# A DiT step on one core: the tiles that matmuls stream are placed at multiples of 64 bytes in SBUF

## The chip, the core and the metric

The kernel runs on one core of one Trainium2 chip, and nothing else runs on the other cores. The metric is device time in microseconds (us) of one launch. The time before is 2669.81 us, the median of 3 runs (2667.17 to 2671.09). TensorE (PE in the profile) multiplies. VectorE (DVE), ScalarE (ACT) and GpSimd (POOL) do the elementwise work. Every DMA is issued from SyncE's queue (SP). SBUF is the on-chip memory with 128 partitions. "The address" of a tile below is the byte in each partition at which it starts.

## What is computed

One layer of a diffusion backbone works on 128 context tokens and 2048 latent tokens of width 1024, everything in float32. The parts that matter here are the input projection and the MLP.

```python
def block(x, s0, mod, ...):
    sh1, sc1, ga1, sh2, sc2, ga2 = mod
    h = rmsnorm(x, norm_mix_l) * (1.0 + sc1) + sh1
    o, s_new = mixer(h, s0, n_chunks, w_in_l, ...)   # h @ w_in, conv, DeltaNet scan, gMLP, @ w_out
    x = x + ga1 * o
    h = rmsnorm(x, norm_ffn_l) * (1.0 + sc2) + sh2
    x = x + ga2 * (jnp.square(jax.nn.relu(h @ w_ff1_l)) @ w_ff2_l)   # 1024 -> 4096 -> 1024
    return x, s_new
```

A final RMSNorm follows. The outputs are both token streams and the last DeltaNet states.

## The kernel before

**Products.** TensorE multiplies float32 data in the type fp32r, in one pass. To keep float32 precision, both operands are split into a high and a low part, and `mm3` (lines 221 to 227) issues three matmuls for each product: high by high (L225), high by low (L226), low by high (L227). In `T.matmul(ps, a, b)` the tile `a` is loaded into the array as the stationary operand, and the tile `b` is streamed. The profile writes a matmul as `out<-streamed,stationary`, so `f<-hop,zH` streams a tile called `hop` past the stationary tile `zH`, and `pj<-kH,wH` streams `kH` past `wH`.

**Stages.** By the first matmuls of each kind in the profile's timeline there are four stages.

- Up to about 520 us, the input projection for q, k and v in feature layout. Tokens go in six blocks: block 0 has 388 columns, blocks 1 to 4 have 386, block 5 has 258. `prep_block` makes for each of the 8 slices of the width a tile `kH` and a tile `kL` (lines 483 and 484): the modulated rows, high and low part. `feature_tile` streams their first 388, 386 or 258 columns against the weights `wH`, `wL`, and `ab_block` (L625, L626) streams them against `abW`.
- From there to 1279 us, the DeltaNet scan, its triangular inverses in float16 (`unit`, L1041 to L1120), the gMLP and the output projection. The tiles of the inverses (`AH`, `X`, `Y`, `P`, `R`) lie in the pool `prep`.
- From 1279.42 to 1991 us, the first MLP product. Rows and columns are combined in the way of Strassen, so that 7 block products take the place of 8. The order is `ORDER = (1, 5, 6, 7, 3, 2, 4)`. `Unit.product` (L1526) issues for each of 32 units and each product 4 x 3 matmuls that stream one `hop` tile: four runs of 128 columns, 4 KB apart.
- From 1991.11 us to the end, the second MLP product, again with 7 products. Each output unit `u` goes through four quarters `q` of the inner dimension, each quarter with one `hop` tile and 4 x 3 matmuls of 512 columns in a row (the loop at L1874).

**Where the tiles lie.** Two pools hold the `hop` tiles, which are 16 KB per partition. `hopA` has 2 of them at the right end of SBUF, where the pool `prep` lay before it (`swap_right`, L1355); `hopB` has 5 of them, just behind the pool `wp`. `hop_tile` (L932) chooses the pool:

```python
def hop_tile(dt, n):
    side, bufs = ("A", 2) if n else ("B", 5)
```

In the first MLP product, products 1 and 5 use hopA (L939: `o in ORDER[:2]`). In the second, of the 28 `hop` tiles that are built one after another, the first two of every five use hopA (L1649). Those are quarters 0 and 1 of the first product, 1 and 2 of the second, 2 and 3 of the third, 3 of the fourth, 0 of the fifth, 0 and 1 of the sixth, 1 and 2 of the last.

A tile's room is rounded up to 32 bytes. A `kH` or `kL` tile of 388 columns has 1552 bytes and takes 1568, which is 24.5 times 64, so every second one starts 32 bytes past a multiple of 64. The right end of SBUF itself lies 32 bytes past a multiple of 64, and so does every tile of hopA and of `prep`. In the built program the addresses, taken modulo 64, are:

| tiles | before | after |
|---|---|---|
| `hop` of hopA (2 places; 16 of the 42 streamed `hop` tiles) | 32 | 0 |
| `hop` of hopB (5 places; 26 of the 42) | 0 | 0 |
| `kH`, `kL` of block 0 | 0, 32 | 0, 0 |
| `kH`, `kL` of blocks 1 to 4 | half of the tiles 0, half 32 | 0, 0 |
| `kH`, `kL` of block 5 | 32, 0 | 0, 0 |
| `AH`, `AL`, `X`, `Y`, `P`, `R`, `E`, `Es`, `KK` of `prep` | 32 | 0 |
| `wsT`, a stationary operand (L1248) | 32 | 0 |
| everything in `wp`, the other streamed tiles | 0 | 0 |

The two places of hopA are bytes 196576 and 212960 before, 196544 and 212928 after. Those of hopB are 113024, 129408, 145792, 162176 and 178560 in both.

The order of the instructions on each engine is worked out when the kernel is built.

Of the kernel before, what the change touches and what calls it, by code (L numbers as in the profile page):

```python
# [8 lines left out]
F32 = mybir.dt.float32  # L9
F32R = mybir.dt.float32r  # L10
# [7 lines left out]
P = 128  # L18
# [44 lines left out]
def hybrid_step(  # L63
# [11 lines left out]
    def xrow(t):  # L75
        return x_prompt[0] if t == 0 else x_sample[0, (t - 1) * P : t * P, :]
# [7 lines left out]
    def f32(ap):  # L84
        return ap.bitcast(F32)

    cp = ctx.enter_context(tc.tile_pool(name="const", bufs=1))
# [19 lines left out]
    def by_tiles(dst, tiles):  # L107

        return dst[tiles].rearrange("a p d -> p a d")
# [8 lines left out]
    make_identity(nc, ident)  # L118
    ident16 = cp.tile([P, P], F16, name="ident16")
    V.tensor_copy(ident16, ident)  # L120
    nhalf = cp.tile([P, 72], F32, name="nhalf")
    V.memset(nhalf, -0.5)
    zcol = cp.tile([P, KT], F32, name="zcol")
    V.memset(zcol, 0.0)
# [42 lines left out]
    wsT = cp.tile([P, 4, P], F32, name="wsT")  # L167
    scond = cp.tile([P, KT, 2], F32, name="scond")

    smp = ctx.enter_context(tc.tile_pool(name="small", bufs=4, reuse_waits="tile"))  # L170
    wp = ctx.enter_context(tc.tile_pool(name="wp", bufs=49, reuse_waits="tile"))
    wst = ctx.enter_context(ExitStack())
# [5 lines left out]
    def rsqrt_cols(out, ss, n, scale, eps):  # L178
        t = smp.tile([P, 72], F32, tag="rsq", name="rsq", bufs=2)
        np_ = ss.shape[0]  # L180
        V.tensor_scalar(out=t[:np_, :n], in0=ss, scalar1=scale, scalar2=eps, op0=ALU.mult, op1=ALU.add)  # L181
        G.tensor_tensor(out=out, in0=t[:np_, :n], in1=nhalf[:np_, :n], op=ALU.pow)  # L182
# [43 lines left out]
            T.matmul(ps, lh, rl, start=False, stop=False, skip_group_check=more)  # L226
            T.matmul(ps, ll, rh, start=False, stop=last and i == n - 1, skip_group_check=more)  # L227

    pick = smp.tile([P, 2, 2], F32, tag="pick", name="pick", bufs=1)
    V.memset(pick, 0.0)  # L230
    V.memset(pick[:, 0, 0:1], 1.0)
    V.memset(pick[:, 1, 1:2], 1.0)
# [42 lines left out]
    with ExitStack() as ph:  # L275
        p1 = ph.enter_context(tc.tile_pool(name="p1", bufs=2, reuse_waits="tile"))
# [7 lines left out]
        def pt():  # L284
            return ppt.tile([P, 512], F32, tag="pt", name="pt", bufs=3)
# [139 lines left out]
        def prep_block(bi):  # L425

            tiles = BLOCKS[bi]
            n = len(tiles) * P
            if bi == 0:
                ncol, segs = 388, [(1, 0, P, 0), (131, P, 2 * P, 1)]  # L430
            else:
                ncol, segs = n + 2, [(1, 0, n, 1)]
            hH, hL = [], []
            c0 = tiles[0] * P
            xs = []

            def load_x(t):
                if bi == 0:
                    xs.append(xs0[t])
                    return  # L440
                x = p1.tile([P, D], F32, tag="x", name="x", bufs=3)
                load(out=x, in_=xrow(t))
                if t == tiles[0]:
                    xs.append(smp.tile([P, 3], F32, tag="ss3", name="xss"))
                i = t - tiles[0]
                junk = p1.tile([P, D], BF16, tag="junk", name="junk", bufs=1)
                A.activation(junk, x, AF.Square, accum_out=xs[0][:, i : i + 1])

            def columns_r():
                nt = len(tiles)  # L450
                r = smp.tile([P, 3], F32, tag="rk", name="xr")
                rsqrt_cols(r[:, :nt], xs[0][:, :nt], nt, 1.0 / D, EPS)
                diag = p1.tile([P, 3, P], F32, tag="diag", name="diag", bufs=1)
                V.tensor_tensor(out=diag[:, :nt, :], in0=ident.unsqueeze(1).to_broadcast([P, nt, P]),
                                in1=r[:, :nt].unsqueeze(2).to_broadcast([P, nt, P]), op=ALU.mult)
                xs.append(diag)

            def rows_r():

                pr = pt()  # L460
                T.matmul(pr[:, :n], ones, xs[1][:, : len(tiles), :].rearrange("p a b -> p (a b)"), start=True,
                         stop=True)
                xs[1] = p1.tile([P, 384], F32, tag="rrow", name="rrow", bufs=1)
                A.copy(xs[1][:, :n], pr[:, :n])

            pairs = []

            def load_pair(j):
                x = p1.tile([P, D], F32, tag="x", name="xT", bufs=3)
                x = x[:, : 2 * n].rearrange("p (k t) -> p k t", k=2)  # L470
                load(out=x, in_=x_columns.rearrange("(k p) t -> p k t", p=P)[:, 2 * j : 2 * j + 2, c0 - P : c0 - P + n])
                pairs.append(x)

            zc, hc = [], []
            if bi == 0:
                zc, hc = [0, 129, 130], [(387, 1)]
            elif bi == 5:
                zc, hc = [n + 1], [(0, 8)]
            else:
                hc = [(0, 2 * bi - 2), (n + 1, 2 * bi + 1)]  # L480
            def column(k):
                full = p1.tile([P, 384], F32, tag="full", name="full", bufs=2)
                kH = p1.tile([P, 388], F32R, tag="h", name="kH", bufs=24)
                kL = p1.tile([P, 388], F32R, tag="h", name="kL", bufs=24)
                for col in zc:
                    G.tensor_copy(kH[:, col : col + 1], zcol[:, 0:1])
                    G.tensor_copy(kL[:, col : col + 1], zcol[:, 0:1])
                for col, j in hc:
                    G.tensor_copy(kH[:, col : col + 1], f32(halH)[:, k, j : j + 1])
                    G.tensor_copy(kL[:, col : col + 1], f32(halL)[:, k, j : j + 1])  # L490
                if bi == 0:
                    ps = pt()
                    for i, x in enumerate(xs):
                        T.transpose(ps[:, i * P : (i + 1) * P], x[:, k * P : (k + 1) * P], ident)
                    for s, o, m, cd in segs:
                        A.activation(full[:, o : o + m], ps[:, o : o + m], AF.Identity,
                                     scale=a1[:, cd, k : k + 1], bias=b1[:, cd, k : k + 1])
                    for s, o, m, _ in segs:
                        V.tensor_copy(kH[:, s : s + m], full[:, o : o + m])
                        V.tensor_tensor(out=kL[:, s : s + m], in0=full[:, o : o + m], in1=f32(kH)[:, s : s + m],  # L500
                                        op=ALU.subtract)
                else:
                    if k == 2:
                        load_pair(3)
                    b = b1[:, 1, k : k + 1]
                    V.scalar_tensor_tensor(out=full[:, :n], in0=pairs[k // 2][:, k % 2, :], scalar=a1[:, 1, k : k + 1],
                                           in1=xs[1][:, :n], op0=ALU.mult, op1=ALU.mult)
                    A.activation(kH[:, 1 : n + 1], full[:, :n], AF.Identity, bias=b)
                    V.scalar_tensor_tensor(out=kL[:, 1 : n + 1], in0=full[:, :n], scalar=b,
                                           in1=f32(kH)[:, 1 : n + 1], op0=ALU.add, op1=ALU.subtract)  # L510
                for s, o, m, _ in segs:
                    at = slice(tiles[0] + o // P, tiles[0] + (o + m) // P)
                    for dst, src in ((hH_d, kH), (hL_d, kL)):
                        store(out=by_tiles(dst[:, :, k, :], at),
                              in_=f32(src)[:, s : s + m].rearrange("p (a d) -> p a d", d=P))
                hH.append(kH)
                hL.append(kL)
            blk = (hH, hL, ncol, segs)
            first = [lambda t=t: load_x(t) for t in tiles]
            if bi:  # L520
                first += [lambda: (columns_r(), load_pair(0)), lambda: (rows_r(), load_pair(1)), lambda: load_pair(2)]
            return blk, first, [lambda k=k: column(k) for k in range(KT)]

        def feature_tile(blk, bi, gi, h):
# [250 lines left out]
        side = []  # L775
        for bi in range(len(BLOCKS)):
# [8 lines left out]
            for n, (gi, h) in enumerate(order):  # L785
# [40 lines left out]
                side = []  # L826
# [117 lines left out]
    with ExitStack() as ph:  # L944
        right = ctx.enter_context(ExitStack())
# [928 lines left out]
    for m, (n, i, u, q) in enumerate(todo):  # L1874
# [12 lines left out]
        h, lo = sops.pop(m)  # L1887
# [70 lines left out]
```

## Time and profile before

| | |
|---|---|
| time, median of 3 runs | 2669.81 us (2667.17 to 2671.09) |
| span of the profiled execution | 2670.2 us |
| mean granted TensorE clock | 0.994 |
| PE busy | 98% |
| PEld (weight loads, beside the matmuls) busy | 82% |
| DVE, ACT, POOL busy | 67%, 47%, 9% |
| DMA queue, share of 16 engines | 67.1% |

In the rows of the profile, `| 376.5, 393 | 1.2 <-ACT zH L1474 1.2` means 376.5 us busy in all, 393 ns for the mean of one instruction, and 1.2 us idle before them, which ended when ACT had written `zH`. A matmul's 393 ns runs from its start to the end of its last write. The next one starts before that, so the pace of a stream of matmuls is the distance from start to start, which the timeline shows. Lines such as `1285.04 0.39 PE L225 ...` give the start in us from the start of the span, and the duration.

### The profile page before, as it was taken

How to read it: one execution, taken by the hardware profiler on the slowest of the kernel's cores; microseconds unless marked ns; L12 is line 12 of the kernel's file. 1: busy time of each engine (PE TensorE's matmuls, PEld its weight loads, DVE VectorE, ACT ScalarE, POOL GpSimd, SP SyncE). 2: the span in 40 equal slices, each digit the busy share in tenths (PEclk: the TensorE clock that was granted, in tenths of full speed). 3: DMA queues.
4: the chain of work that ended last, by engine and by line, in shares of the span. 5: the costliest groups of instructions: out<-in, count | busy, mean ns of one | idle time of the engine just before them, and what ended most of it. 6: DMA issues, size and time to landing. Idle time of an engine off the chain costs nothing.

```text
span 2670.2 us, 45051 instructions
## 1 busy us (share of the span) xinstructions
PE 2625.4 (98%) x15714; PEld 2192.3 (82%) x15714; DVE 1790.4 (67%) x3694; ACT 1245.7 (47%) x3092; POOL 230.1 (9%) x448
## 2 busy tenths in 40 slices
PE   9999999999999999999999999999999999999998
PEld 5999998787887777788888888888888787888887
DVE  5867655766666778875677885556565556774874
ACT  4755555655555657763455543333242432332441
POOL 3111213111111111110000000000000000000000
PEclk9999999999999999999999999999999999999999
DMA  8967638654445657875877786343369979786782
GB/s 290 295 200 225 185 109 285 199 163 151 154 159 167 211 182 259 293 269 178 288 221 233 251 298 215 108 125 103 109 197 372 328 263 310 263 255 206 234 260 89
DMA packets 499753, 580.89 MB, mean 218 GB/s; under 512 B 35692, under 2 KB 298268, under 8 KB 495942
## 3 DMA queue, kind: packets, MB, share of 16 engines
q1 hardware_dynamic: 499526, 578.03, 67.1%
q8 instruction: 123, 2.02, 0.3%
q14 instruction: 104, 0.85, 0.1%
HBM read 398.14 MB, written 179.74 MB: 216 GB/s over the span
## 4 chain that ended last, share of the span: by engine, by line
PE 86%; DMA 6%; DVE 4%; ACT 2%; issue 1%; POOL 1%; SPq 0%; DVEq 0%; POOLq 0%; ACTq 0%
PE f L227 17%; PE f L225 17%; PE f L226 17%; PE pj L225 7%; PE pj L227 6%; PE pj L226 6%; PE pd L991 3%; PE pm L225 1%; PE pm L227 1%; PE pm L226 1%; DMA raw<-in_w_mod_dram 1%; DMA qT<-qT_d 1%; PE pd L1164 1%; PE pd L1165 1%; PE pt L605 1%
## 5 line engine op out<-in xcount | busy, mean ns | idle before, releaser
L225 PE MATMUL f<-hop,zH 128*128 128x512 f32 x960 | 376.5, 393 | 1.2 <-ACT zH L1474 1.2
L226 PE MATMUL f<-hop,zH 128*128 128x512 f32 x960 | 377.1, 393 | 0.0
L227 PE MATMUL f<-hop,zL 128*128 128x512 f32 x960 | 376.9, 393 | 0.0
L225 PE MATMUL f<-hop,wH 128*128 128x512 f32 x896 | 354.1, 396 | 0.3 <-issue 0.3
L226 PE MATMUL f<-hop,wH 128*128 128x512 f32 x896 | 350.7, 391 | 0.0
L227 PE MATMUL f<-hop,wL 128*128 128x512 f32 x896 | 350.0, 392 | 0.0
L1474 ACT CAST zH<-zraw 128x512 fp32r<-128x512 f32 x240 | 146.8, 620 | 298.8 <-DMA zraw<-s_d 89.2
L225 PEld LDWEIGHTS f<-hop,zH 128*128 128x128 f32 x960 | 180.4, 188 | 43.7 <-ACT zH L1474 1.6
L227 PEld LDWEIGHTS f<-hop,zL 128*128 128x128 f32 x960 | 180.3, 188 | 41.9 <-issue 0.9
L226 PEld LDWEIGHTS f<-hop,zH 128*128 128x128 f32 x960 | 180.2, 188 | 41.8 <-issue 0.9
L1468 DVE TENSOR_TENSOR zL<-zraw,zH 128x512 fp32r<-128x512 f32 x240 | 162.8, 687 | 69.0 <-ACT zH L1474 53.9
L227 PEld LDWEIGHTS f<-hop,wL 128*128 128x128 f32 x896 | 168.3, 188 | 37.6
L226 PEld LDWEIGHTS f<-hop,wH 128*128 128x128 f32 x896 | 168.5, 188 | 35.4
L225 PEld LDWEIGHTS f<-hop,wH 128*128 128x128 f32 x896 | 168.4, 188 | 35.4 <-issue 0.7
L225 PE MATMUL pj<-kH,wH 128*128 128x386 f32 (+2 forms) x568 | 190.5, 338 | 2.0 <-ACT junk L581 1.1
L227 PE MATMUL pj<-kH,wL 128*128 128x386 f32 (+2 forms) x568 | 189.7, 334 | 0.0
L226 PE MATMUL pj<-kL,wH 128*128 128x386 f32 (+2 forms) x568 | 188.9, 334 | 0.0
L182 POOL TENSOR_TENSOR r<-rsq,nhalf 128x1 f32<-128x1 f32 (+1 forms) x38 | 24.1, 633 | 1471.7 <-DVE rsq L181 1471.7
L1468 DVE TENSOR_TENSOR wL<-raw,wH 128x512 fp32r<-128x512 f32 x112 | 76.1, 687 | 76.4 <-ACT wH L1474 75.5
L551 DVE SCALAR_TENSOR_TENSOR cv<-pj,vec,cv 128x384 f32<-128x384 f32 (+2 forms) x164 | 87.0, 539 | 54.8 <-ACT cv L548 53.6
L225 PEld LDWEIGHTS pj<-kH,wH 128*128 128x128 f32 x568 | 107.0, 189 | 7.7 <-issue 4.7
L1474 ACT CAST wH<-s 128x512 fp32r<-128x512 f32 x96 | 59.3, 620 | 105.5 <-DVE s L1468 105.2
(403 smaller groups left out, 6048.3 us busy)
## 6 DMA issues: line engine op xcount, KB each, us to landing
zraw<-z_d SPq DMA_DIRECT2D x212, 256.0 KB
raw<-in_w_ff_dram SPq DMA_DIRECT2D x128, 256.0 KB
hop<-hop_d SPq DMA_DIRECT2D x28, 1024.0 KB
z_d<-c SPq DMA_DIRECT2D x96, 256.0 KB
zraw<-s_d SPq DMA_DIRECT2D x96, 256.0 KB
raw<-in_w_mod_dram SPq DMA_DIRECT2D x80, 256.0 KB
r<-in_w_ff_dram SPq DMA_DIRECT2D x80, 256.0 KB
s_d<-s SPq DMA_DIRECT2D x64, 256.0 KB
```

Source lines behind the costliest of these rows:

```text
L182: G.tensor_tensor(out=out, in0=t[:np_, :n], in1=nhalf[:np_, :n], op=ALU.pow)
L225: T.matmul(ps, lh, rh, start=first and i == 0, stop=False, skip_group_check=more)
L226: T.matmul(ps, lh, rl, start=False, stop=False, skip_group_check=more)
L227: T.matmul(ps, ll, rh, start=False, stop=last and i == n - 1, skip_group_check=more)
L551: V.scalar_tensor_tensor(out=cv[:, o : o + m], in0=ps[:, s + sh : s + sh + m], scalar=convw[:, w, j : j + 1], in1=cv[:, o : o + m], op0=AL ...
L605: T.matmul(ps[:, i * P : (i + 1) * P], kTt[:, i * P : (i + 1) * P], rhs[:, i * P : (i + 1) * P], start=True, stop=True)
L991: T.matmul(p[:, h, :], lhs[:, h, :], rhs[:, h, :], start=True, stop=True)
L1164: T.matmul(p[:, h, :], u["qT"][:, h, :], s[:, h, :], start=True, stop=False)
L1165: T.matmul(p[:, h, :], u["QK"][:, h, :], u["vn"][:, h, :], start=s is None, stop=True)
L1468: V.tensor_tensor(out=out, in0=a, in1=b, op=op)
L1474: A.copy(h, src)
```

## The change

The right end of SBUF gets a pool of its own, `edge`, with the 16-byte tile `pick`, which moves there from the pool `small`. It takes 32 bytes, and the pools on that side that come after it (`prep`, then `hopA`) lie 32 bytes lower. `nhalf` grows from 72 to 80 columns, that is by 32 bytes, so that the pools behind the constants stay where they were while the constants in between move up by 32 bytes. `kH` and `kL` become 400 columns wide, 1600 bytes or 25 times 64; the columns that are written and streamed stay the same.

```diff
-    nhalf = cp.tile([P, 72], F32, name="nhalf")
+    nhalf = cp.tile([P, 80], F32, name="nhalf")
...
+    edge = ctx.enter_context(tc.tile_pool(name="edge", bufs=1, side="right"))
     smp = ctx.enter_context(tc.tile_pool(name="small", bufs=4, reuse_waits="tile"))
...
-    pick = smp.tile([P, 2, 2], F32, tag="pick", name="pick", bufs=1)
+    pick = edge.tile([P, 2, 2], F32, name="pick")
...
-                kH = p1.tile([P, 388], F32R, tag="h", name="kH", bufs=24)
-                kL = p1.tile([P, 388], F32R, tag="h", name="kL", bufs=24)
+                kH = p1.tile([P, 400], F32R, tag="h", name="kH", bufs=24)
+                kL = p1.tile([P, 400], F32R, tag="h", name="kL", bufs=24)
```

The order does not change: row by row each engine and the DMA queue have the same instructions in the same order, with the same tiles and shapes, but for the 80 columns of `nhalf`'s fill. What differs is the addresses, and the lists of semaphores that six instructions of the first units of the inverses wait for (two of POOL at L1019 and L1021, four of DVE at L1035 and L1044), because `prep` now overlaps other tiles of the stage before it.

## The prediction

> **What bounds the kernel now.** I read the page first, for the engine that carries the span, then the waits of PE in the two MLP stages, then the sums by stage. From the page:
>
> ```profile
> PE 2625.4 (98%) x15714; PEld 2192.3 (82%) x15714; DVE 1790.4 (67%) x3694; ACT 1245.7 (47%) x3092; POOL 230.1 (9%) x448
> PE 86%; DMA 6%; DVE 4%; ACT 2%; issue 1%; POOL 1%; SPq 0%; DVEq 0%; POOLq 0%; ACTq 0%
> PE f L227 17%; PE f L225 17%; PE f L226 17%; PE pj L225 7%; PE pj L227 6%; PE pj L226 6%; PE pd L991 3%; PE pm L225 1%; PE pm L227 1%; PE pm L226 1%; DMA raw<-in_w_mod_dram 1%; DMA qT<-qT_d 1%; PE pd L1164 1%; PE pd L1165 1%; PE pt L605 1%
> L225 PE MATMUL f<-hop,zH 128*128 128x512 f32 x960 | 376.5, 393 | 1.2 <-ACT zH L1474 1.2
> L225 PE MATMUL f<-hop,wH 128*128 128x512 f32 x896 | 354.1, 396 | 0.3 <-issue 0.3
> ```
>
> PE is busy nearly always and holds 86% of the chain that ended last; 51% of the span is the three lines of `mm3` that write `f`, the MLP. They come 3 x (960 + 896) = 5568 times. All the waits of PE from 1290 us to the end, and the sums of three stretches:
>
> ```profile
> PE f L225 <- ACT zH L1474: 1.2, 1, 1.2
> PE f L225 <- issue: 0.3, 1, 0.3
> 1279.00:1950.00 671.00, 670.67 (x3315) 562.72 (x3314) 456.47 (x745) 268.39 (x530) 5.65 (x9) 1.00 0.63 197
> 1950.00:2670.00 720.00, 710.22 (x3106) 575.95 (x3105) 456.96 (x741) 247.29 (x455) 11.74 (x17) 1.00 0.76 254
> 2000.00:2040.00 40.00, 40.00 (x175) 32.49 (x174) 19.99 (x31) 9.84 (x17) 0.00 (x0) 1.00 1.02 367
> ```
>
> In 1380 us PE waits 1.5 us for others, at a full granted clock (1.00). So each nanosecond that one MLP matmul takes less is a nanosecond of the span, as long as the DMA keeps up; its share is 0.63 and 0.76 in the mean and full (1.02) only in a stretch like 2000 to 2040 us.
>
> **Does the start of a streamed tile matter?** The trace answers, because hopA's tiles start 32 bytes past a multiple of 64 and hopB's on one. In the first MLP product the first two units run together, 24 matmuls on each `hop` tile: product 1 (hopA) from 1279.42, product 7 (hopB) from 1296.69, product 3 (hopB) from 1302.13. In the second MLP product the quarters of one output unit, 12 matmuls each, are hopA, hopA, hopB (its lowest place, byte 113024), hopB (178560). The rows are the first matmul of each stretch and the first behind it:
>
> ```profile
> 1279.42 0.40 PE L225 MATMUL f<-hop,wH 128*128 128x512 f32 x1
> 1285.04 0.39 PE L225 MATMUL f<-hop,wH 128*128 128x512 f32 x1
> ...
> 1296.69 0.39 PE L225 MATMUL f<-hop,wH 128*128 128x512 f32 x1
> 1302.13 0.39 PE L225 MATMUL f<-hop,wH 128*128 128x512 f32 x1
> 1307.57 0.39 PE L225 MATMUL f<-hop,wH 128*128 128x512 f32 x1
> ```
>
> ```profile
> 2002.24 0.40 PE L225 MATMUL f<-hop,zH 128*128 128x512 f32 x1
> 2005.06 0.39 PE L225 MATMUL f<-hop,zH 128*128 128x512 f32 x1
> 2007.86 0.40 PE L225 MATMUL f<-hop,zH 128*128 128x512 f32 x1
> 2010.61 0.39 PE L225 MATMUL f<-hop,zH 128*128 128x512 f32 x1
> 2013.33 0.40 PE L225 MATMUL f<-hop,zH 128*128 128x512 f32 x1
> ```
>
> First stage: 5.62 / 24 = 234.2 ns for one matmul on hopA, 5.44 / 24 = 226.7 ns on hopB, twice. Second stage: 2.82 and 2.80 us for a quarter on hopA, 2.75 on the lowest hopB tile, 2.72 on the higher one. So the offset tiles cost some 7 ns for a matmul.
>
> Whether the same holds for the `kH` and `kL` tiles needs their rows. Block 0 (388 columns) has `kH` on a multiple of 64 and `kL` 32 past one; block 5 (258) the other way round:
>
> ```profile
> L226 PE MATMUL pj<-kL,wH 128*128 128x388 f32 x88 | 30.0, 344 | 0.0
> L227 PE MATMUL pj<-kH,wL 128*128 128x388 f32 x88 | 29.9, 342 | 0.0
> L225 PE MATMUL pj<-kH,wH 128*128 128x388 f32 x88 | 29.2, 345 | 1.9 <-ACT junk L581 1.1 <-POOL kH L489 0.8
> L227 PE MATMUL pj<-kH,wL 128*128 128x258 f32 x96 | 27.9, 291 | 0.0
> L225 PE MATMUL pj<-kH,wH 128*128 128x258 f32 x96 | 27.7, 288 | 0.0
> L226 PE MATMUL pj<-kL,wH 128*128 128x258 f32 x96 | 27.4, 286 | 0.0
> ```
>
> ```profile
> 100.41 0.33 PE L225 MATMUL pj<-kH,wH 128*128 128x388 f32 x1
> ...
> 102.53 0.33 PE L225 MATMUL pj<-kH,wH 128*128 128x388 f32 x1
> ```
>
> ```profile
> 420.81 0.28 PE L227 MATMUL pj<-kH,wL 128*128 128x258 f32 x1
> ...
> 422.26 0.28 PE L227 MATMUL pj<-kH,wL 128*128 128x258 f32 x1
> ```
>
> At 388 columns the offset `kL` takes 344 ns between 342 and 345: no difference. At 258 the offset `kH` takes 2 to 5 ns more than `kL`. From start to start, twelve matmuls take 2.12 us at 388 columns (176.7 ns each) and 1.45 at 258 (120.8).
>
> These numbers fit one rule. Count the pieces of 64 bytes, at multiples of 64, that a streamed row touches: 512 columns (2048 bytes) touch 32 from a multiple of 64 and 33 from 32 past it; 388 columns (1552 bytes) touch 25 from either, and so do 386; 258 (1032 bytes) touch 17 from either. Then 226.7 / 32, 234.2 / 33, 176.7 / 25 and 120.8 / 17 are 7.08, 7.10, 7.07 and 7.11 ns for one piece. It is a fit and not a proof. In the first MLP product the row is four runs of 512 bytes; counted apart, those would touch 36 pieces from an offset start, and 234.2 speaks for 33, as if they joined.
>
> **The change part by part.**
>
> 1. hopA to a multiple of 64: the gain. Matmuls that stream hopA: 2 products x 32 units x 12 = 768 in the first MLP stage, and 18 + 16 + 16 + 9 + 9 + 16 + 18 = 102 quarters x 12 = 1224 in the second (eight output units for a product, nine where the context tile is one of them). Together 1992, or 166 groups of 12. At one piece (7.1 ns) less for each: 14.1 us. From both sides: 2.82 to 2.72 for a group gives 16.6 us, 2.80 to 2.72 gives 13.3, and if the shifted tiles ran like the slow hopB tile, from 2.81 to 2.75, it were 10.0. I take 14.1. No wait takes its place that the rows show: the next matmul's operands were there already, but for 1.2 us.
>
> 2. `kH`, `kL` 400 columns apart: nothing. Of 1824 matmuls on them (3 x 576, and 96 more in `ab_block`), half, 912, start at an offset now: 104 of block 0, 608 of blocks 1 to 4, 200 of block 5. By pieces none changes. The bounds are the 5 ns between the rows at 258 columns, either way: 912 x 5 = 4.6 us less or more, on a stage where PE sets the pace.
>
> 3. `prep` and `wsT` to multiples of 64: nothing. Of the float16 matmuls, `Y` (offset) streamed past `AH` takes 219 ns and `ident16` (on a multiple) past `X` 223; the weight load of `wsT` (offset) takes 191 ns and that of `QK` (on a multiple) 192:
>
> ```profile
> L1109 PE MATMUL pd<-Y,AH 128*128 128x128 f16 x136 | 18.9, 219 | 0.2 <-DVE Y L1102 0.2
> L1041 PE MATMUL pd<-ident,X 128*128 128x128 f16 x136 | 13.6, 223 | 2.8 <-DVE X L1035 2.1 <-DVE S L1153 0.7
> L1248 PEld LDWEIGHTS pm<-vg,wsT 128*128 128x128 f32 x104 | 13.5, 191 | 0.9
> L1165 PEld LDWEIGHTS pd<-vn,QK 128*128 128x128 f32 x272 | 40.9, 192 | 0.1
> ```
>
> The offset one is the faster of the first two; their 4 ns over the 272 matmuls of both rows are 1.1 us, either way.
>
> 4. The rest costs nothing that I can find: `nhalf`'s fill writes 8 columns more once, `pick` only moves, and the changed waits come once, at the stage's start, for tiles that were stored long before.
>
> Sum: 2670.2 - 14.1 = 2656.1 us by the profiled execution, which lies 0.4 above the median. I forecast **2656 us**.
>
> **A rule that speaks against it.** The Trainium skill (SBUF — State Buffer, Specifications (TRN2)) gives SBUF lines of 16 bytes as what an access pays for. By it a start at 32 past a multiple of 64 is the start of a line, term 1 is nothing, and the time stays 2670. The trace does not agree as far as pool and offset can be told apart: 234.2 against 226.7 ns.
>
> **The rivals.**
>
> - *It is the place, not the offset.* In the trace all offset `hop` tiles lie in hopA, at the top of SBUF, and they stay there; if 234 ns comes from where they lie, nothing changes: 2670. For it: hopB's tiles differ too (2.75 against 2.72), with no offset at all. Against it: the higher hopB tile is the faster, and the count of pieces fits four lengths.
> - *The unit is finer or coarser than 64.* With pieces of 16 or 32 bytes the offset was no offset, with 128 the new places (64 past a multiple of 128) are still offset: 2670 in both cases. For it: nothing but that no `hop` tile stands at such a place now. Against it: with pieces of 128 bytes the lengths touch 16, 13 and 9, which gives 14.2, 13.6 and 13.4 ns each, no constant.
> - *The `k` tiles gain as well.* The 5 ns of block 5 are the offset after all: 2656.1 - 4.6 = 2651.5. Against it: block 0.
> - *The transfers take part of it.* Where the DMA share is full (1.02), faster quarters run ahead of their loads. The first product of the second MLP stage has 18 hopA quarters x 0.085 us = 1.5 us; if the whole second stage were so, its 102 x 0.085 = 8.7 us are lost: 2664.8. Against it: 0.76 in the mean.
> - *Slower: tiles on the same residue collide.* The weights that load meanwhile lie at multiples of 64, and after the change every streamed tile does. If that costs a piece (7.1 ns) on the 912 `k` matmuls, they lose 6.5 us, and hopA, meeting the same weights, gains nothing: 2676.7. With the gain of hopA kept, it would have to cost over 14.1 us / 912 = 15 ns to end above. For it: `kL` at 388 columns, offset, is no slower than its neighbours. Against it: hopB and the weights are both on multiples, at 226.7 ns, the fastest there is.
>
> **How the numbers follow.** The forecast has 71% (2653 to 2661), the `k` gain as well 8% (about 2651), the transfers 6% (2661 to 2665), place 6% and unit 4% (both 2670), slower 5% (2677). The range from 2650 to 2665 holds the first three and their bounds and leaves out 15% and a little at its lower end. A measurement of this kernel tells about 0.2%, 5.3 us, from no change, so faster means under 2664.5: 0.84. Within 0.2%: 0.11, place and unit and an edge of the transfers. Slower: 0.05.
>
> **What would show it.** Right: a quarter on hopA takes 2.72 us from first start to first start, all mean durations of `f` on 512 columns come down from 393 to near 390, the rows of `pj<-kH` stay within 5 ns, and the span from 1279 us to the end shrinks by 14 us while everything before it shifts by under 6. Wrong: hopA still at 2.81 us (place or unit); new waits of PE for `zH` or `zL` that a DMA ends (transfers); `pj` rows that change by more than 5 ns.

## The result, and the profile after

| | before | after |
|---|---|---|
| time, median of 6 runs each | 2668.31 us (2665.95 to 2671.09) | 2657.21 us (2653.82 to 2664.13) |
| ratio, 95% interval | | 0.9961 (0.9951 to 0.9971) |
| span of the profiled execution | 2670.2 us | 2662.4 us |
| first MLP matmul to the end, in it | 1390.7 us | 1384.0 us |

The change made the kernel faster by 11 us, 0.4%. The profiled execution of after happens to be the slowest of its six. The spans of these six go from 2652.1 us at a mean granted clock of 0.997 to 2662.4 at 0.994, so most of that spread goes with the clock, and stages are compared below by the MLP alone, where it is full (1.00 in the profile's stretches).

From the page of after, first the span, then the share of PE and the chain of waits, which still run through the same three lines (now L226 to L228, one further down):

```profile
span 2662.4 us, 45053 instructions
PE 2616.4 (98%) x15714; PEld 2191.3 (82%) x15714; DVE 1789.6 (67%) x3694; ACT 1245.9 (47%) x3092; POOL 230.6 (9%) x448
PE 85%; DMA 6%; DVE 4%; ACT 2%; issue 1%; SPq 1%; POOL 1%; DVEq 0%; POOLq 0%; ACTq 0%
```

The groups of the second MLP stage (mean ns of one is the number after the comma), and all waits of PE from 1290 us on:

```profile
L226 PE MATMUL f<-hop,zH 128*128 128x512 f32 x960 | 377.1, 393 | 1.2 <-ACT zH L1475 1.2
L228 PE MATMUL f<-hop,zL 128*128 128x512 f32 x960 | 375.6, 392 | 0.0
L227 PE MATMUL f<-hop,zH 128*128 128x512 f32 x960 | 373.6, 390 | 0.0
```

```profile
PE f L226 <- ACT wH L1475: 1.2, 1, 1.2
PE f L226 <- ACT zH L1475: 1.2, 1, 1.2
```

PE still waits for next to nothing, 2.4 us. The means came down by 0 to 3 ns, to 390 to 393, and not to 390 on all three lines. The pace of a stream is in the starts. The timeline of after: the first matmul of the MLP, the first of its second stage, and then the four quarters of the second output unit (hopA, hopA, the lowest place of hopB, a higher place of hopB) with the first matmul behind them:

```profile
1278.44 0.40 PE L226 MATMUL f<-hop,wH 128*128 128x512 f32 x1
...
1988.11 0.45 PE L226 MATMUL f<-hop,zH 128*128 128x512 f32 x1
...
1999.13 0.40 PE L226 MATMUL f<-hop,zH 128*128 128x512 f32 x1
2001.89 0.39 PE L226 MATMUL f<-hop,zH 128*128 128x512 f32 x1
2004.64 0.40 PE L226 MATMUL f<-hop,zH 128*128 128x512 f32 x1
2007.41 0.39 PE L226 MATMUL f<-hop,zH 128*128 128x512 f32 x1
2010.13 0.40 PE L226 MATMUL f<-hop,zH 128*128 128x512 f32 x1
```

A quarter on hopA takes 2.76 and 2.75 us, where it took 2.82 and 2.80, and not the 2.72 that the higher hopB tile takes. The lowest hopB tile takes 2.77, no better than before. The first MLP stage went from 711.7 to 709.7 us (1279.42 to 1991.11 before), the second from 679.0 to 674.3: 6.8 us in all. So the gain is where it was expected, and hopA got two thirds of the way in its pace.

The rows of the `k` tiles, for two of the three lengths, moved by 3 ns at most:

```profile
L228 PE MATMUL pj<-kH,wL 128*128 128x388 f32 x88 | 30.0, 343 | 0.0
L227 PE MATMUL pj<-kL,wH 128*128 128x388 f32 x88 | 29.9, 344 | 0.0
L226 PE MATMUL pj<-kH,wH 128*128 128x388 f32 x88 | 29.2, 344 | 2.1 <-ACT junk L582 1.1 <-POOL kH L490 1.0
L228 PE MATMUL pj<-kH,wL 128*128 128x258 f32 x96 | 27.7, 288 | 0.0
L226 PE MATMUL pj<-kH,wH 128*128 128x258 f32 x96 | 27.5, 287 | 0.0
L227 PE MATMUL pj<-kL,wH 128*128 128x258 f32 x96 | 27.5, 286 | 0.0
```

Two questions are left: why hopA stopped at 2.75 us, and whether offset, place or something else decides.

### The profile page after: what moved, and what is told of

Read it like the earlier page. It is cut to its first block, busy times and chain, and to the rows that moved or that the text cites. A ratio compares the mean times of both kernels' runs of the same rounds, so it can differ in the third digit from the quotient of the medians.

```text
span 2662.4 us, 45053 instructions
## 1 busy us (share of the span) xinstructions
PE 2616.4 (98%) x15714; PEld 2191.3 (82%) x15714; DVE 1789.6 (67%) x3694; ACT 1245.9 (47%) x3092; POOL 230.6 (9%) x448
## 4 chain that ended last, share of the span: by engine, by line
PE 85%; DMA 6%; DVE 4%; ACT 2%; issue 1%; SPq 1%; POOL 1%; DVEq 0%; POOLq 0%; ACTq 0%
PE f L226 17%; PE f L228 17%; PE f L227 17%; PE pj L226 6%; PE pj L228 6%; PE pj L227 6%; PE pd L992 3%; PE pm L226 1%; DMA raw<-in_w_mod_dram 1%; PE pm L228 1%; PE pm L227 1%; PE pd L1165 1%; PE pd L1166 1%; PE pt L606 1%; DMA qT<-qT_d 1%
## 5 line engine op out<-in xcount | busy, mean ns | idle before, releaser
L226 PE MATMUL f<-hop,zH 128*128 128x512 f32 x960 | 377.1, 393 | 1.2 <-ACT zH L1475 1.2
L228 PE MATMUL f<-hop,zL 128*128 128x512 f32 x960 | 375.6, 392 | 0.0
L226 PE MATMUL f<-hop,wH 128*128 128x512 f32 x896 | 353.8, 396 | 1.2 <-ACT wH L1475 1.2
L228 PE MATMUL f<-hop,wL 128*128 128x512 f32 x896 | 348.9, 391 | 0.0
L228 PEld LDWEIGHTS f<-hop,zL 128*128 128x128 f32 x960 | 180.2, 188 | 42.4 <-issue 0.9
L226 PEld LDWEIGHTS f<-hop,zH 128*128 128x128 f32 x960 | 180.3, 188 | 40.1 <-ACT zH L1475 1.6
L228 PEld LDWEIGHTS f<-hop,wL 128*128 128x128 f32 x896 | 168.2, 188 | 37.1
L226 PEld LDWEIGHTS f<-hop,wH 128*128 128x128 f32 x896 | 168.4, 188 | 35.2 <-ACT wH L1475 1.6
L226 PE MATMUL pj<-kH,wH 128*128 128x386 f32 (+2 forms) x568 | 189.7, 337 | 2.3 <-ACT junk L582 1.1
L228 PE MATMUL pj<-kH,wL 128*128 128x386 f32 (+2 forms) x568 | 189.5, 334 | 0.0
L226 PEld LDWEIGHTS pj<-kH,wH 128*128 128x128 f32 x568 | 107.0, 189 | 7.9 <-issue 4.7
```

The source lines that it names most:

```text
L226: T.matmul(ps, lh, rh, start=first and i == 0, stop=False, skip_group_check=more)
```

## The experiments

In all of them but the one with 386 columns, the instructions of PE, DVE, ACT and the DMA queue stand in the same order as in after, and those of POOL too but for five places in the kernels that move `wp`; only addresses differ. "Three matmuls" means the distance from start to start of the three of one `mm3`, the median over the last two of the four products on a tile, taken from the timeline: 700 ns on hopA and 680 on hopB before, 687 and 680 after.

### One part at a time

The right end alone, with `kH` and `kL` 388 columns wide again:

```diff
-                kH = p1.tile([P, 400], F32R, tag="h", name="kH", bufs=24)
-                kL = p1.tile([P, 400], F32R, tag="h", name="kL", bufs=24)
+                kH = p1.tile([P, 388], F32R, tag="h", name="kH", bufs=24)
+                kL = p1.tile([P, 388], F32R, tag="h", name="kL", bufs=24)
```

> Only the right end of SBUF moves by 32 bytes (hopA and prep on multiples of 64); kH and kL stay 388 columns wide, half of them offset. Theory (hopA's start is the whole gain): as the full change, ratio to before 0.996, and 12 matmuls on hopA at the same pace as in the full change (about 2.74 us a quarter). Rival (the k tiles gain too): a part of the gain is missing, up to 4.6 us, ratio 0.9975 or more.

Measured: 2660.55 us, ratio 0.9978 (0.9968 to 0.9988). Three matmuls on hopA take 687 ns, and the MLP takes 1383.8 us, as in the full change (1384.0).

The width alone, from the kernel before:

```diff
-                kH = p1.tile([P, 388], F32R, tag="h", name="kH", bufs=24)
-                kL = p1.tile([P, 388], F32R, tag="h", name="kL", bufs=24)
+                kH = p1.tile([P, 400], F32R, tag="h", name="kH", bufs=24)
+                kL = p1.tile([P, 400], F32R, tag="h", name="kL", bufs=24)
```

> Only kH and kL become 400 columns wide; hopA stays 32 bytes past a multiple of 64. Theory: no change, ratio 1.000, pj rows within 5 ns of before, a quarter on hopA still 2.80 us. Rival (k gains): 2 to 5 us less, ratio 0.998 to 0.999. Rival (same residue collides): up to 6.5 us more, ratio 1.0024.

Measured: 2668.34 us, ratio 0.9999 (0.9990 to 1.0008); 700 ns on hopA, the MLP 1390.3 us. The width alone does nothing that the time can tell, and the right end carries all that the MLP gained. The right end alone came out 0.0017 above the full change, with intervals that overlap by little. In the profiled executions the MLP is the same in both, and the difference lies before it (the MLP starts at 1281.4 us against 1278.4), where the clock also varies. The width has a small part in that: over the products that follow one another without a break, three matmuls on the `k` tiles take 530.6 ns in the mean in place of 532.1 at 386 columns and 357.7 in place of 362.1 at 258, after against before, and the other traces with tiles of these two widths agree closely. With 384 and 96 such products that is an estimated 1.0 us, less than the times can tell.

### 64 bytes further, and hopB moved

```diff
+    edge.tile([P, 16], F32, name="pad")
     pick = edge.tile([P, 2, 2], F32, name="pick")
```

> The full change with 64 bytes more at the right end: hopA starts on multiples of 128 (196480, 212864), as hopB does, where the full change has it 64 past one. Three matmuls of a product on hopA take 687 ns from start to start after the change, those on the upper hopB tiles 680 to 681. If multiples of 128 are what matters for the rest: 680 on hopA too, 166 x 4 x 7 ns = 4.6 us less than the full change, ratio to before 0.994. If hopA's place (the top of SBUF) costs the rest: 687 stays, ratio 0.996 as the full change.

Measured: 2652.10 us, ratio 0.9939 (0.9926 to 0.9951); beside a later kernel again 2652.75 us, 0.9940 (0.9927 to 0.9953).

> e3_right_96 once more, beside e6_k_128: ratio to before 0.994, within 0.001.

This version beats both kernels, the changed one by 5 us. The same rows of its timeline as above, without the start of the second stage:

```profile
1276.14 0.39 PE L226 MATMUL f<-hop,wH 128*128 128x512 f32 x1
...
1994.15 0.39 PE L226 MATMUL f<-hop,zH 128*128 128x512 f32 x1
1996.87 0.39 PE L226 MATMUL f<-hop,zH 128*128 128x512 f32 x1
1999.59 0.39 PE L226 MATMUL f<-hop,zH 128*128 128x512 f32 x1
2002.31 0.39 PE L226 MATMUL f<-hop,zH 128*128 128x512 f32 x1
2005.03 0.39 PE L226 MATMUL f<-hop,zH 128*128 128x512 f32 x1
```

All four quarters take 2.72 us, the lowest hopB tile too, whose address is what it always was. It had been slow only because it follows a hopA tile: in the kernel before, its first nine matmuls were slower, on the way from 700 to 680 ns for three, its last three not. The MLP takes 1376.3 us (to the end at 2652.4), 14.4 less than before. So a multiple of 64 was not enough, and the top of SBUF is as good a place as any.

The other way round: hopA as in the change, hopB 32 bytes off.

```diff
+    pad = ctx.enter_context(tc.tile_pool(name="padB", bufs=1))
+    pad.tile([P, 8], F32, name="padB")
     hops["B"] = ctx.enter_context(tc.tile_pool(name="hopB", bufs=1, reuse_waits="tile"))
```

> The full change, but hopB starts 32 bytes past a multiple of 64 (113056 and so on); hopA stays on a multiple. hopB carries 5568 - 1992 = 3576 matmuls. If the offset costs one piece of 64 bytes (7.1 ns) wherever the tile lies: three matmuls on hopB go from 681 to 700 ns or more, 3576 x 7.1 = 25 us more than the full change, ratio to before 1.005. If the place was the cause and not the offset: hopB stays at 681, ratio 0.996.

Measured: 2676.70 us, ratio 1.0031 (1.0019 to 1.0042). Quarters of the second unit, in the order of the rows above:

```profile
2004.58 0.40 PE L226 MATMUL f<-hop,zH 128*128 128x512 f32 x1
2007.34 0.39 PE L226 MATMUL f<-hop,zH 128*128 128x512 f32 x1
2010.08 0.40 PE L226 MATMUL f<-hop,zH 128*128 128x512 f32 x1
2012.88 0.39 PE L226 MATMUL f<-hop,zH 128*128 128x512 f32 x1
2015.68 0.39 PE L226 MATMUL f<-hop,zH 128*128 128x512 f32 x1
```

hopB takes 2.80 us a quarter, 700 ns for three, at the places where it took 2.77 and 2.72. The pace goes with the address. The cost is smaller than expected, though: the MLP takes 1400.6 us, 16.6 more than after, where 25 was worked out. A part of that is plain in the rows: a hopB quarter behind a hopA one took 2.77 us in after already, so it loses 0.03 us and not 0.08.

### Starts of every kind

Each `hop` tile with its own start:

```diff
-        return hops[side].tile([P, 4, 2, 4, P], dt, tag="hop", name="hop", bufs=bufs)
+        o = STARTS[len(made) % len(STARTS)]
+        made.append(o)
+        t = hops[side].tile([P, 4128], dt, tag="hop", name="hop", bufs=bufs)
+        return t[:, o : o + 4096].rearrange("p (a b c d) -> p a b c d", a=4, b=2, c=4)
...
+    made = []
+    STARTS = (0, 1, 2, 4, 8, 12, 16, 20, 24, 28)
```

> Each hop tile gets 128 bytes more room, and its data begin 0, 4, 8, 16, 32, 48, 64, 80, 96 or 112 bytes past a multiple of 128, in turn from tile to tile. So far three matmuls of one product take 680 ns at 0, 687 at 64, 700 to 702 at 32 and at 96. Theory (the read goes in blocks of 128 bytes, of which a half costs little): 16, 48, 80 and 112 take 700 to 702 too, 4 and 8 as well or more. Rival (blocks of 16 bytes decide, as lines): 16, 48, 80, 112 do not differ from 32, and only 4 and 8 are slower than all others. Rival (pieces of 64 bytes alone): 0 and 64 alike, all others 700. Whole time between the full change and 2675 us.

Measured: 2692.53 us (one run). Tiles change every 12 matmuls here and hardly settle, so the 0 mostly shows as 684 to 685. Three matmuls at 16 and 48: about 699 ns; at 32: 700; at 64: 687; at 80 and 112: 693; at 4 and 8, starts that are no multiple of 16, anything from 700 to 731, unlike from tile to tile. So a start 16 bytes off costs as much as one 32 off. None of the three accounts covers this: 80 and 112 are neither as 32 nor as 64.

Then `kH` and `kL` on multiples of 128, on top of the version with 64 bytes more:

```diff
-                kH = p1.tile([P, 400], F32R, tag="h", name="kH", bufs=24)
-                kL = p1.tile([P, 400], F32R, tag="h", name="kL", bufs=24)
+                kH = p1.tile([P, 416], F32R, tag="h", name="kH", bufs=24)
+                kL = p1.tile([P, 416], F32R, tag="h", name="kL", bufs=24)
...
-            sb = p1.tile([32, 384], F32, tag="absb", name="absb", bufs=1)
+            sb = p1.tile([P, 384], F32, tag="rrow", name="absb", bufs=1)[0:32, :]
```

> As e3_right_96, and kH and kL 416 columns wide, so that they start on multiples of 128 (the tile absb takes the room of rrow, to make space). All tiles that matmuls stream then start on multiples of 128. Theory (64 past a multiple of 128 costs something on the k tiles too): three matmuls of 386 columns take less than the 529 and 535 ns that they take with one of kH and kL 64 past, some 520; 576 x 10 ns = 6 us less than e3_right_96, ratio to before 0.992. Rival (386 columns are 25 pieces of 64 from either start, so nothing changes): 529 to 535 stay, ratio as e3_right_96, 0.994.

Measured: 2652.15 us, ratio 0.9937 (0.9923 to 0.9950): as the version without it. Three matmuls of 386 columns take 528.6 ns in the mean, against 530.6, where some 520 was worked out, and at 258 columns they take more, 364.9 against 357.7; over 384 and 96 products the two nearly cancel. A miss for the theory.

### Which operand

So far the stationary tiles, all in `wp`, had not moved. Now they do, by 32 bytes; the `hop` tiles stay where the best version has them.

```diff
-    nhalf = cp.tile([P, 80], F32, name="nhalf")
+    nhalf = cp.tile([P, 88], F32, name="nhalf")
...
+    pad = ctx.enter_context(tc.tile_pool(name="padB", bufs=1))
+    pad.tile([P, 24], F32, name="padB")
     hops["B"] = ctx.enter_context(tc.tile_pool(name="hopB", bufs=1, reuse_waits="tile"))
```

> As e3_right_96, but all tiles of wp (in the MLP the stationary operands) lie 32 bytes past a multiple of 128, and the hop tiles stay on multiples. Theory (only the streamed tile's start matters): three matmuls on hop stay at 680 to 681 ns. Rival (what matters is the streamed start against the stationary one): 687 to 700. In the stages before the MLP the tiles wH and wL of wp are streamed, 3 x 680 matmuls, and the k tiles are 32 off too: there the time grows by 10 to 20 us against e3_right_96 by the theory.

Measured: 2687.36 us (one run), and an MLP of 1409.5 us. The same quarters in the timeline, and one row of the weight loads by line:

```profile
2009.61 0.40 PE L226 MATMUL f<-hop,zH 128*128 128x512 f32 x1
2012.41 0.40 PE L226 MATMUL f<-hop,zH 128*128 128x512 f32 x1
2015.21 0.40 PE L226 MATMUL f<-hop,zH 128*128 128x512 f32 x1
2018.01 0.39 PE L226 MATMUL f<-hop,zH 128*128 128x512 f32 x1
2020.81 0.40 PE L226 MATMUL f<-hop,zH 128*128 128x512 f32 x1
```

```profile
L226 PEld LDWEIGHTS f<-hop,zH 128*128 128x128 f32 x923 | 173.4, 188 | 43.9 <-ACT zH L1478 2.5
```

Every quarter takes 2.80 us, with all `hop` tiles on multiples of 128. The start of the streamed tile by itself is not the cause. The weight load shows the same 188 ns as before. And the stages before the MLP did not get slower: it begins at 1276.18 us, against 1276.14 in the best version, although 3 x 680 matmuls stream tiles of `wp` there. Their stationary tiles had moved by the same 32 bytes. That leaves the difference of the two starts. The test is to move both:

```diff
-    edge.tile([P, 16], F32, name="pad")
+    edge.tile([P, 8], F32, name="pad")
...
-    pad = ctx.enter_context(tc.tile_pool(name="padB", bufs=1))
-    pad.tile([P, 24], F32, name="padB")
```

> All tiles of wp and all hop tiles lie 32 bytes past a multiple of 128, so that streamed and stationary operands have the same start modulo 128. Theory (what costs is that the streamed and the stationary operand start at different places modulo 128): three matmuls on hop take 680 to 681 ns again, as in e3_right_96, and the time is 0.994 of before. Rival (each operand has to start on a multiple of 64 by itself): 700 ns or more, ratio 1.004 or more.

Measured: 2653.75 us, ratio 0.9939 (0.9922 to 0.9956).

```profile
1996.84 0.39 PE L226 MATMUL f<-hop,zH 128*128 128x512 f32 x1
1999.56 0.39 PE L226 MATMUL f<-hop,zH 128*128 128x512 f32 x1
2002.28 0.39 PE L226 MATMUL f<-hop,zH 128*128 128x512 f32 x1
2005.00 0.39 PE L226 MATMUL f<-hop,zH 128*128 128x512 f32 x1
2007.72 0.39 PE L226 MATMUL f<-hop,zH 128*128 128x512 f32 x1
```

2.72 us in every quarter, with not one tile that the MLP's matmuls read on a multiple of 64. The theory holds: what counts is that the streamed and the stationary operand start at the same place. To find the modulus, the difference was made 64 and then 128. From the kernel with the weights 32 off:

```diff
-    nhalf = cp.tile([P, 88], F32, name="nhalf")
+    nhalf = cp.tile([P, 96], F32, name="nhalf")
...
-    pad.tile([P, 24], F32, name="padB")
+    pad.tile([P, 16], F32, name="padB")
```

> All tiles of wp lie 64 bytes past a multiple of 128, all hop tiles on multiples: the full change's relation of 64 bytes, with the operands swapped and on all seven places. Theory (the difference of the starts decides): three matmuls on hop take 687 ns, everywhere, after a few of settling. Rival (only the streamed operand's 64 costs): 680. About 2660 us by the theory, 2652 by the rival.

Measured: 2670.74 us (one run), 10 us above what was worked out. Its quarters, again hopA, hopA, hopB, hopB:

```profile
2000.92 0.39 PE L226 MATMUL f<-hop,zH 128*128 128x512 f32 x1
2003.71 0.40 PE L226 MATMUL f<-hop,zH 128*128 128x512 f32 x1
2006.51 0.39 PE L226 MATMUL f<-hop,zH 128*128 128x512 f32 x1
2009.26 0.39 PE L226 MATMUL f<-hop,zH 128*128 128x512 f32 x1
2012.01 0.39 PE L226 MATMUL f<-hop,zH 128*128 128x512 f32 x1
```

hopB takes 2.75 us (687 for three), as expected, but hopA takes 2.79 and 2.80 (700). Modulo 128 both are 64 apart from `wp`; modulo 256 hopB is 64 and hopA 192 past it. So the modulus is more than 128. From the best version, 128 apart everywhere:

```diff
-    edge.tile([P, 16], F32, name="pad")
+    edge.tile([P, 48], F32, name="pad")
...
+    pad = ctx.enter_context(tc.tile_pool(name="padB", bufs=1))
+    pad.tile([P, 32], F32, name="padB")
```

> All hop tiles start 128 bytes past the place that the stationary tiles have modulo 256 (hop at multiples of 256, wp at 128 past one). So far the difference streamed minus stationary, modulo 256, gave for three matmuls: 0: 680 ns, 64: 687, 192: 700, 32, 96 and 224: 700. Theory (the difference counts modulo 256, as 64 and 192 are unlike): 128 apart is a place of its own, 687 to 700, and the time lies 5 to 25 us above that of e3_right_96 (2652). Rival (it counts modulo 128, and 192 was slow for another reason): 680, time 2652.

Measured: 2682.56 us, ratio 1.0042 (1.0028 to 1.0056). The same quarters:

```profile
2008.61 0.40 PE L226 MATMUL f<-hop,zH 128*128 128x512 f32 x1
2011.39 0.40 PE L226 MATMUL f<-hop,zH 128*128 128x512 f32 x1
2014.18 0.39 PE L226 MATMUL f<-hop,zH 128*128 128x512 f32 x1
2016.97 0.39 PE L226 MATMUL f<-hop,zH 128*128 128x512 f32 x1
2019.75 0.40 PE L226 MATMUL f<-hop,zH 128*128 128x512 f32 x1
```

A quarter takes 2.78 or 2.79 us here. Three matmuls never settle on one value: they go back and forth between 690 and 705 ns on all seven places, 699 in the mean of the second stage. 128 apart is slow too. Streamed start minus stationary start, modulo 256, over the settled runs:

| difference, bytes | 0 | 32 | 64 | 96 | 128 | 192 | 224 |
|---|---|---|---|---|---|---|---|
| three matmuls of 512 columns, ns | 680 | 700 | 687 | 700 | 699 (690 to 705) | 700 | 700 |

In the kernel with starts of every kind, tiles that differ by 256 more agree (0 and 256, 64 and 320, 80 and 336, 112 and 368 give the same within 1 ns). At 8 bytes past a multiple of 128 they do not: in the second stage 136 gives 707 and 392 gives 700 to 706, so 256 is shown as the modulus for multiples of 16 only. No settled `hop` tile at 0 was slow in any run, and none at another difference was as fast.

### Fewer columns

```diff
-        mm3(ps, [(h[:, kp, :], lo[:, kp, :], t[:, 0, :], t[:, 1, :])
-                 for kp, t in enumerate(tiles[n][4 * q : 4 * q + 4])], first=q == 0, last=q == 3)
+        for kp, t in enumerate(tiles[n][4 * q : 4 * q + 4]):
+            th, tl = (t[:, j].rearrange("p a d -> p (a d)") for j in range(2))
+            c = slice(0, 512 if q == kp == 0 else 386)
+            mm3(ps[:, c], [(h[:, kp, :], lo[:, kp, :], th[:, c], tl[:, c])], first=q == kp == 0,
+                last=q == kp == 3, more=True)
```

> The kernel before, but the matmuls of the second MLP stage stream only 386 of the 512 columns (but for the first one of each output unit); the products of columns 386 to 511 are left out. hopA is 32 bytes past a multiple of 64, hopB on one. Theory (a stream of 386 columns does not feel the offset, which is why the k tiles gained nothing): three matmuls take 530 to 537 ns on hopA and on hopB alike. Rival (offset tiles are slower at any length, and the k tiles are hidden by something else): hopA 13 to 20 ns above hopB.

This kernel, made from the one before, leaves out the products of columns 386 to 511. Measured: 2558.34 us (one run). Three matmuls take 540 ns on hopA and 529 on hopB, medians, in a stage that now often waits for its loads. Neither account: once the pace has settled the offset costs 11 ns at 386 columns, about half of the 20 at 512. Behind a wait hopA also runs at 520 for a while, so that the means, without the waits, are 532 and 529.

## Why the prediction was right

The forecast of the time came out, but of the signs that the prediction named two did not: a quarter on hopA takes 2.75 us and not 2.72, and the MLP shrank by 6.8 us and not by 14. The mean durations came down to 390 on one line of three. The `pj` rows within 5 ns and the small shift before the MLP, 1.0 us, are as it said.

1. *What bounds the kernel.* Right: PE sets the pace of the MLP, with 1.5 us of waits before and 2.4 after. The faster pace of the best version arrived in the span: its MLP is 14.4 us shorter, and its time 15.8 us in the medians. No transfer took anything back, and that rival falls.

2. *hopA, 14.1 us.* The place and the sign were right, the size and the reason were not. The MLP gave 6.8 us. The step that failed is "These numbers fit one rule. Count the pieces of 64 bytes": four paces (three lengths, one of them from two starts) fitted 7.1 ns for one piece, but the streamed tile's pieces are not what costs. With all `hop` tiles on multiples of 128 and the weights 32 bytes off, three matmuls took 700 ns; with both 32 off, 680. The two pools of the kernel before differed in their distance from `wp`, and the change brought hopA from 96 to 64 bytes modulo 256, where the pace is 687, and not to 0. With 64 bytes more the MLP gives 14.4 us, so the term's number was that of an edit that was not made.

3. *The bound of 10.0 us*, from a "slow hopB tile", read a transient as a place: that tile was slow because it followed hopA, and it takes 2.72 us where hopA does.

4. *`kH`, `kL`: nothing.* Right in size: 0.9999 alone, and 1.0 us by the pace of the products. The reason given, 25 pieces from either start, falls with the rule. The trace of after says what stands in its place only in part: with a tile pitch of 1600 bytes the differences from the weights go round through 0, 64, 128 and 192, so most stayed off 0, and at 386 columns an offset costs half as much or less. On multiples of 128 they are 0 and 128 apart in turn. All of them at 0 was not tried, since 24 tiles with a pitch of 1792 bytes do not fit beside the rest; but at 386 columns hopB at 0 took 529 ns, and the `k` tiles take 530.6 already, so little seems left there.

5. *`prep` and `wsT`: nothing.* Nothing speaks against it; the stages before the MLP ended between 1274 and 1283 us in all profiled runs, with no order by their addresses.

6. *The rivals.* "Place" is out (hopA runs at 680 in its place, hopB at 700 in its own). "Unit" was right in that 64 is too fine, but wrong in that nothing would be gained. "Tiles on the same residue collide" is the opposite of what is so: the same residue is the fast case. The Trainium skill's lines of 16 bytes (SBUF — State Buffer, Specifications (TRN2)) do not explain the pace: 16 and 48 bytes, whole lines, cost 699 against 680. The Trainium skill's statement that the loading of weights takes no read bandwidth from the running matmul (TensorE: Matmul & The Clock Gate, Step-by-step: what each phase is for) does not lead one to expect what was measured: moving the weights alone by 32 bytes cost 20 ns for three matmuls and 33 us of MLP. Whether the two reads compete is not shown by any run here.

The forecast of 2656 us met 2657.21 partly by luck. The MLP accounts for 6.8 us of a difference of 11.1 in the medians. The profiled pair differs by 1.0 us more before the MLP, about what the pace of the `k` products gives. The other 3.3 us are the difference between that pair and the medians, in launches whose clock varies; which stage they come from is not known.

## What to carry to other kernels

Compare matmuls by the distance from start to start, tile by tile, since the mean duration hid a 3% difference in pace. Where TensorE sets the end and streams fp32r against weights that change with every matmul, place the streamed and the stationary tiles at the same address modulo 256 bytes, and measure it: here, at 512 columns, 64 bytes of padding were worth 5 us. A pattern fitted on one layout may name the wrong operand; move the other one before believing it.

## What the runs showed of the hardware that was not expected

- The pace of the MLP's matmuls (fp32r, 512 columns, a weight load for each) depends on where the streamed operand starts against the stationary one: 680 ns for three at a difference of 0 modulo 256 bytes, 687 at 64, 699 in the mean at 128, 700 at 32, 96, 192 and 224. Why is open; the record of the weight load stays at 188 or 189 ns.
- A change of pace can take nine matmuls or more to settle: a tile with 0 difference behind one with 96 runs its first nine at 690 to 695 ns for three and its last three at 680; behind one with 64 the last three still take 684. From 0 to 64 three matmuls are enough.
- The mean granted clock differs from launch to launch of one kernel, 0.994 to 0.997 here, and with it the span by 10 us of 2660.
